# Down-projection of a convolutional FFN: where the residual sums, the bank reads and the operand sums are done

## The chip, the core and the metric

The kernel runs on one core of a Trainium2 chip. The metric is the device time of one execution in microseconds. Engines are called PE (TensorE), DVE (VectorE), ACT (ScalarE) and POOL (GpSimd); SP is the queue that issues the DMAs.

## What is computed

The program is one transformer layer on 1024 tokens of 1024 features. A Hyena mixer comes first, then the FFN of this case. Cut to what matters here:

```python
def conv_ffn(u, w_up, conv_w, conv_b, w_down, rows, cols):
    a, g = jnp.split(u @ w_up, 2, axis=-1)
    g = grid_dwconv(g, conv_w, conv_b, rows, cols)
    return (jax.nn.silu(g) * a) @ w_down
...
x = x + g2 * conv_ffn(modulate(rmsnorm(x, norm_g[i, 1]), sh2, sc2), *ffn_p, rows, GRID_W)
return rmsnorm(x, final_g)
```

The hidden width is 2816. All of it is float32: each float32 operand is split into a high and a low part, and a product is three matmuls.

## The kernel before, in words

The last stage, `ffn_down`, multiplies the hidden activations u (2816 x 1024 tokens, kept in DRAM as `du`) by w_down (2816 x 1024, `in_ffn_w_down_dram`). The product is made with seven block products instead of eight (the Strassen-Winograd scheme). Tokens, output features and the 2816 rows of the contraction are each cut in two halves. A product P1 to P7 runs over k = 0 to 10, blocks of 128 contraction rows, and for each k over four groups j of 128 tokens. So a step (p, k) is 4 x 3 = 12 matmuls of 128x128 by 128x512, and the stage has 77 steps. Four PSUM banks `bA` (named dA in the trace) take P1, P6, P7 and P4 one after the other; four banks `bB` (dB) take P2, P5 and P3. P6, P7 and P4 add onto what stands in bA: after P1 and P6 it is the sum called U2 here, after P7 it is U3, and P4 is added to that. So U2 and U3 have to be read out of bA before the next product changes it. The four quarters of the output are C11 (P1 + P2), C12 (U2 + P5 + P3; P3 is added onto P5 in bB), C22 (U3 + P5) and C21 (U3 + P4). In words of the code: C11 and C12 make tokens 0 to 511 (lo and hi features), C21 and C22 make tokens 512 to 1023.

The order of the steps is `dseq`, written out in `down_start`. P1 and P2 are mixed, then P6 and P5, then P7 k 0 and 1, P3 mixed with P7 k 2 to 4, P7 k 5 to 10, and P4. For every step, `down_load` issues DMAs from SP into a ring of raw tiles `dr` (13 tiles early, 11 from P5 k 7 on, 7 for P4), and `down_prep` makes the operands:

- for P5 it adds two tiles on POOL (line 1176), subtracts two on DVE (line 1177), and after the split writes two cached sums c for later products (lines 1203 and 1204);
- for P7 it makes one difference on POOL (line 1185) and one on DVE (line 1186); for P3 one on DVE (line 1189); for P4 one on POOL (line 1192);
- then `split` rounds each operand to its high part dh on ACT (line 62) and subtracts to get the low part dl on DVE (line 63).

A raw tile is free for the next DMA when its last reader is done. All the queues are in order: an instruction that waits holds those behind it on the same engine. The order on each engine is set by a scheduler when the program is built, not by the order of the lines alone.

The other work of the stage is the output. When a product is complete its banks are read: P1 to tiles p1 and P6 to tiles u2 by ACT (line 1300 for U2), P5 to tiles p5 by ACT (line 1304), P2, P3 and P7 by DVE, each adding the part stored before (lines 1307, 1315 and 1311). Then small jobs follow, popped one by one between the steps: `c11` multiplies by the gate g2 and adds the residual x1, both on POOL (line 1245, eight instructions); `c22` does the same for C22 on POOL (lines 1256 and 1251) with a square and its row sum on ACT; `c12` does it for C12 on DVE (lines 1265 and 1266) with squares on ACT (line 1268), then a mean, a reciprocal root (`rstd`, lines 354 to 362) and the final scaling (line 1276) with the output DMA. The tail is C21: for the last four k of P4 the loop runs j by j, and after each j DVE multiplies the bank by g2 (line 1332), adds the residual (line 1333), ACT squares, `rfin` makes the reciprocal root and DVE scales 1024 columns (line 1340) for a 512 KB output DMA; the last j is scaled in two halves, one on ACT (line 1343), one on DVE (line 1345).

Of the kernel before, what the change touches and what calls it, by code (L numbers as in the profile page):

```python
# [47 lines left out]
class Kern:  # L48
# [1167 lines left out]
    def ffn_down(self):  # L1216
# [30 lines left out]
        def c22(j, t):  # L1247
            y = lambda: self.x1[4 + j][:, hi]

            def last():  # L1250
                gt(out=y(), in0=y(), in1=t, op=ALU.add)
                self.sq(4 + j, 1, y(), t)
                if j == 3:
                    gt(out=y(), in0=y(), in1=fg[:, hi], op=ALU.mult)

            return [lambda: gt(out=t, in0=t, in1=g2[:, hi], op=ALU.mult), last]
# [24 lines left out]
        for n in range(N - LAST):  # L1281
# [37 lines left out]
            if vjobs and n % 3:  # L1319
                vjobs.pop(0)()  # L1320
        while vjobs or gjobs:
            for q in (gjobs, vjobs):
                if q:
                    q.pop(0)()
        for j in range(4):
            for n in range(N - LAST, N):
# [1 line left out]
            t = 4 + j
            y = self.x1[t]
            o = op.tile([128, 512], F32, tag="ot", name=f"dt{j}", bufs=2)  # L1330
            jk = op.tile([128, 512], F32, tag="nt", name=f"dj{j}", bufs=2)
            vt(out=o, in0=self.bA[j], in1=g2[:, lo], op=ALU.mult)  # L1332
            vt(out=y[:, lo], in0=y[:, lo], in1=o, op=ALU.add)  # L1333
            self.sq(t, 0, y[:, lo], jk)
# [2 lines left out]
            r = self.rfin(t)
            dst = a["out"][t * 128:t * 128 + 128]
            if j < 3:
                nc.vector.scalar_tensor_tensor(out=y, in0=y, scalar=r, in1=fg, op0=ALU.mult, op1=ALU.mult)  # L1340
                nc.sync.dma_start(out=dst, in_=y)
                continue
            nc.scalar.activation(out=y[:, hi], in_=y[:, hi], func=AF.Copy, scale=r)
            nc.sync.dma_start(out=dst[:, hi], in_=y[:, hi])
            nc.vector.tensor_scalar(out=y[:, lo], in0=y[:, lo], scalar1=r, scalar2=None, op0=ALU.mult)
            nc.sync.dma_start(out=dst[:, lo], in_=y[:, lo])

    def sq(self, t, h, y, junk):
        if t not in self.ssf:
            self.ssf[t] = self.op.tile([128, 2], F32, tag=f"ss2{t}", name=f"ssf{t}")  # L1350
        self.nc.scalar.activation(out=junk, in_=y, func=AF.Square, accum_out=self.ssf[t][:, h:h + 1])

    def rfin(self, t):
        ss = self.ssf[t]
        s1 = self.op.tile([128, 1], F32, tag="ss1", name=f"sst{t}", bufs=2)
        self.nc.vector.tensor_tensor(out=s1, in0=ss[:, 0:1], in1=ss[:, 1:2], op=ALU.add)
        return self.rstd(s1, 1, f"rf{t}")
# [158 lines left out]
```

## Time and profile before

| | us |
|---|---|
| median of 3 runs | 1305.76 (1305.61 to 1305.9) |
| the profiled execution's own time | 1301.95 |
| its span, first to last instruction | 1300.2 |
| busy: PE, DVE, ACT, POOL | 1232.0, 1063.9, 744.0, 353.2 |
| mean granted TensorE clock | 0.987 of 2.4 GHz |

Times in the rows are microseconds from the start of the span. A row of the timeline has the start, the time from the first start to the last end of the instructions that it merges, the engine, the line, the operation, the tiles written and read, and their count; in square brackets stands how long the engine was idle before, and what ended that. Instructions are pipelined: the next one starts some 0.08 us before the end of the one ahead on DVE, so the pace is a little shorter than the duration. A DMA row of SP shows the issue only. POOL spans are rough.

### The profile page before, as it was taken

What the parts mean: (1) busy time and instruction counts of PE and PEld (TensorE: products, weight loads), DVE (VectorE), ACT (ScalarE), POOL (GpSimd) and SP (SyncE); (2) the same over time, 40 slices, a digit from 0 to 9 for tenths busy, and PEclk for the clock granted to TensorE, in tenths of its full rate; (3) what the DMA queues carried; (4) which work ended last, traced back from release to release, by engine and by line L of the source; (5) the groups of instructions that cost most, each with busy time, mean ns of one, the idle gap of its engine ahead of it and who ended that gap; (6) DMA issues with size and microseconds to landing.
All of it is one profiled execution on the core that took longest, in us unless ns stands there. A gap on an engine that the chain in (4) does not pass through costs nothing. (4 is left out here: it accounts for less than half of the span.)

```text
span 1300.2 us, 16048 instructions
## 1 busy us (share of the span) xinstructions
PE 1232.0 (95%) x5368; PEld 971.7 (75%) x5368; DVE 1063.9 (82%) x1351; ACT 744.0 (57%) x1215; POOL 353.2 (27%) x292
## 2 busy tenths in 40 slices
PE   7999989999899999999989999999999999998976
PEld 2687767777677777878768878888888878886865
DVE  7899875578786998796989998788778798977996
ACT  4798866677676878553644444444544454425442
POOL 2000011012100210000086445455445301521461
PEclk9999999999999999999989999999999999999988
DMA  9555699989989997543124431222222388646542
GB/s 339 191 156 156 209 287 285 275 251 269 270 253 301 273 302 263 175 154 128 51 83 129 161 129 65 98 81 76 87 81 82 130 286 307 232 154 219 197 144 97
DMA packets 112400, 241.35 MB, mean 186 GB/s; under 512 B 12436, under 2 KB 25620, under 8 KB 112318
## 3 DMA queue, kind: packets, MB, share of 16 engines
q1 hardware_dynamic: 96790, 226.83, 53.4%
q0 software_dynamic: 14848, 13.39, 4.9%
q8 instruction: 42, 0.69, 0.2%
q14 instruction: 40, 0.33, 0.1%
q10 hardware_dynamic: 680, 0.12, 0.0%
HBM read 186.29 MB, written 54.00 MB: 185 GB/s over the span
## 5 line engine op out<-in xcount | busy, mean ns | idle before, releaser
L1010 DVE SCALAR_TENSOR_TENSOR facc<-fpad,v_ffn_conv_w,facc 128x1024 f32<-128x1024 f32 x176 | 225.2, 1285 | 22.8 <-ACT facc L1005 19.2
L62 ACT ACTIVATE dh<-dr 128x512 fp32r<-128x512 f32 x132 | 75.7, 623 | 64.0 <-PE dB L58 23.4
L63 DVE TENSOR_TENSOR dl<-dr,dh 128x512 fp32r<-128x512 f32 x132 | 102.8, 825 | 4.2 <-ACT dh L62 4.0
L507 POOL DMA_DIRECT2D k_b<-in_k_b_dram x64 | 34.0, 532 | 263.6 <-PE ks L59 177.3
L973 POOL TENSOR_TENSOR s<-wrua 128x512 f32<-128x512 f32 x21 | 29.3, 1396 | 188.2 <-DVE s12l L963 95.6
L57 PE MATMUL dA<-dh,dh 128*128 128x512 f32 x176 | 69.7, 396 | 8.7 <-DVE p5fpad L1311 7.7
L58 PE MATMUL dA<-dl,dh 128*128 128x512 f32 x176 | 69.2, 393 | 2.0 <-DVE dl L63 2.0
L963 POOL TENSOR_TENSOR s43l<-s,s43h 128x1024 fp32r<-128x1024 f32 x21 | 50.4, 2399 | 68.5 <-ACT s43h L962 68.5
L59 PE MATMUL dA<-dh,dl 128*128 128x512 f32 x176 | 68.9, 392 | 0.0
L58 PE MATMUL dB<-dl,dh 128*128 128x512 f32 x132 | 52.2, 395 | 5.1 <-DVE dl L63 5.1
L59 PE MATMUL dB<-dh,dl 128*128 128x512 f32 x132 | 51.9, 393 | 0.0
L57 PE MATMUL dB<-dh,dh 128*128 128x512 f32 x132 | 51.9, 393 | 0.0
L58 PE MATMUL op<-wlo,qh 128*128 128x512 f32 x128 | 50.3, 393 | 0.0
L57 PE MATMUL op<-who,qh 128*128 128x512 f32 x128 | 50.0, 393 | 0.0
L59 PE MATMUL op<-who,ql 128*128 128x512 f32 x128 | 49.9, 390 | 0.0
L1005 ACT ACTIVATE facc<-fpad,v_ffn_conv_b,v_ffn_conv_w 128x1024 f32<-128x1024 f32 x22 | 26.6, 1210 | 37.4 <-DVE fpad L1073 37.3
L57 PEld LDWEIGHTS dA<-dh,dh 128*128 128x128 f32 x176 | 33.5, 191 | 16.4 <-issue 8.1
L286 DVE SCALAR_TENSOR_TENSOR macc<-mw,scl,macc 128x1024 f32<-128x1024 f32 x28 | 38.1, 1361 | 9.4 <-DMA mw<-in_mod_w_dram 9.2
L507 POOL DMA_DIRECT2D k_bi<-in_k_bi_dram x32 | 17.1, 534 | 103.3 <-PE zd L59 47.6
L962 ACT ACTIVATE s12h<-s 128x1024 fp32r<-128x1024 f32 x21 | 22.3, 1061 | 39.6 <-PE s L58 35.3
L974 POOL TENSOR_TENSOR s<-s,wrug 128x512 f32<-128x512 f32 x21 | 42.8, 2039 | 1.5
L573 ACT ACTIVATE who<-wro,invn 128x512 fp32r<-128x512 f32 x32 | 21.8, 717 | 37.1 <-PE op L59 28.7
(585 smaller groups left out, 4050.4 us busy)
## 6 DMA issues: line engine op xcount, KB each, us to landing
dr<-du SPq DMA_DIRECT2D x66, 256.0 KB, 3.7
dr<-in_ffn_w_down_dram SPq DMA_DIRECT2D x66, 256.0 KB, 4.6
mw<-in_mod_w_dram SPq DMA_DIRECT2D x32, 512.0 KB, 4.6
wrin<-in_hy_w_in_dram SPq DMA_DIRECT2D x24, 512.0 KB, 6.4
wrug<-in_ffn_w_up_dram SPq DMA_DIRECT2D x22, 512.0 KB, 3.4
wrua<-in_ffn_w_up_dram SPq DMA_DIRECT2D x22, 512.0 KB, 4.7
du<-fs SPq DMA_DIRECT2D x22, 512.0 KB, 2.6
mw<-in_mod_w_dram SPq DMA_DIRECT2D x32, 256.0 KB, 6.5
```

The source lines that it names most:

```text
L57: mm(out=out, lhsT=lh, rhs=rh, start=start, stop=False, **kw)
L58: mm(out=out, lhsT=lh, rhs=rl, start=False, stop=False, **kw)
L59: mm(out=out, lhsT=ll, rhs=rh, start=False, stop=stop, **kw)
L62: self.nc.scalar.activation(out=hi, in_=src, func=AF.Copy)
L63: self.nc.vector.tensor_tensor(out=lo, in0=src, in1=hi.bitcast(F32), op=ALU.subtract)
L286: nc.vector.scalar_tensor_tensor(out=acc, in0=w, scalar=self.scl[:, kt:kt + 1], in1=acc, op0=ALU.mult, op1=ALU.add)
L507: self.nc.gpsimd.dma_start(out=b, in_=self.a[name][k2])
L963: eng.tensor_tensor(out=l, in0=src, in1=h.bitcast(F32), op=ALU.subtract)
L973: tt(out=s12[:, lo], in0=a[:, lo], in1=a[:, hi], op=ALU.add)
L974: tt(out=s12[:, hi], in0=s12[:, lo], in1=g[:, lo], op=ALU.subtract)
L1005: nc.scalar.activation(out=av, in_=pad[:, 1:17, 1:65], func=AF.Identity, scale=self.cw[:, b, 4:5], bias=self.cb[:, b:b + 1])
L1010: nc.vector.scalar_tensor_tensor(out=av, in0=pad[:, dy:dy + 16, dx:dx + 64], scalar=self.cw[:, b, i:i + 1], in1=av, op0=ALU.mult, op1=ALU.add)
```

## The change

- The differences of P7 (line 1185) and P4 (line 1192) move from POOL to DVE.
- C11: each group also gets its square (ACT) and its product with the final gain `fg` (POOL) at once: three POOL jobs each, where it was two.
- `pre`: after P6, U2 times g2 and the sum with the residual are done at once on POOL, two instructions for each of four groups; after P5 the same for P5 and a residual half `xh` that is loaded for it.
- P7's and P3's banks are read by the product with g2 (DVE, PSUM and SBUF operands) into a tile of its own, so that the stored first part is not needed at the read; one sum is left for each group, on POOL for C22 and on DVE for C12.
- C12's mean, root and scaling are popped in P4 only; the scaling is half on ACT, half on DVE.
- The tail's `rfin` takes the mean's factor into the square and has five DVE instructions instead of seven; hi halves are scaled by ACT and lo halves by DVE, each with a 256 KB DMA, and the fourth group's chain is put ahead of the third's.
- The residual loads of tokens 512 to 1023 become lo halves (256 KB) and, earlier, hi halves (256 KB).

```diff
         elif p == 7:
             a, b = r[0]
-            gt(out=a, in0=a, in1=self.cache[k][0], op=ALU.subtract)
+            vt(out=a, in0=a, in1=self.cache[k][0], op=ALU.subtract)
             vt(out=b, in0=self.cache[k][1], in1=b, op=ALU.subtract)
...
         else:
             a, b = r[0]
-            gt(out=b, in0=b, in1=self.cache[k][1], op=ALU.subtract)
+            vt(out=b, in0=b, in1=self.cache[k][1], op=ALU.subtract)
...
+        def square(j, h, t):
+            nc.scalar.activation(out=t, in_=self.x1[j][:, (lo, hi)[h]], func=AF.Square, accum_out=ss[:, h, j:j + 1])
+
         def c11(j, t):
             y = self.x1[j][:, lo]
-            return [lambda: gt(out=t, in0=t, in1=g2[:, lo], op=ALU.mult), lambda: gt(out=y, in0=y, in1=t, op=ALU.add)]
...
+            def add():
+                gt(out=y, in0=y, in1=t, op=ALU.add)
+                square(j, 0, t)
+
+            return [lambda: gt(out=t, in0=t, in1=g2[:, lo], op=ALU.mult), add, lambda: gt(out=y, in0=y, in1=fg[:, lo], op=ALU.mult)]
+
+        def pre(t, x, y):
+            return [lambda: gt(out=t, in0=t, in1=g2[:, hi], op=ALU.mult), lambda: gt(out=y, in0=x, in1=t, op=ALU.add)]
+
+        def c22(j, y, t):
+            def add():
+                gt(out=y, in0=y, in1=t, op=ALU.add)
+                self.sq(4 + j, y, t)
+
+            return add, lambda: gt(out=y, in0=y, in1=fg[:, hi], op=ALU.mult)
...
             def first(j):
-                t, y = u2[j], self.x1[j]
-                vt(out=t, in0=t, in1=g2[:, hi], op=ALU.mult)
-                vt(out=y[:, hi], in0=y[:, hi], in1=t, op=ALU.add)
...
+                y = self.x1[j][:, hi]
+                vt(out=y, in0=y, in1=u2[j], op=ALU.add)
+                square(j, 1, u2[j])
...
+            if (p, k) == (5, 7):
+                xh = [op.tile([128, 512], F32, tag=("ot", "nt")[j // 2], name=f"xh{j}", bufs=2) for j in range(4)]
+                for j in range(4):
+                    nc.sync.dma_start(out=xh[j], in_=self.dx[4 + j][:, hi])
...
                     for j in range(4):
                         nc.scalar.activation(out=u2[j], in_=self.bA[j], func=AF.Copy)
+                        y = self.x1[j][:, hi]
+                        gjobs += pre(u2[j], y, y)
                 elif p == 5:
                     p5 = four(("fpad0", "fpad1"), "p5")
                     for j in range(4):
                         nc.scalar.activation(out=p5[j], in_=self.bB[j], func=AF.Copy)
+                        gjobs += pre(p5[j], xh[j], p5[j])
...
                 elif p == 7:
                     for j in range(4):
-                        vt(out=p5[j], in0=self.bA[j], in1=p5[j], op=ALU.add)
-                    gjobs += [f for j in range(4) for f in c22(j, p5[j])]
+                        vt(out=xh[j], in0=self.bA[j], in1=g2[:, hi], op=ALU.mult)
+                    gjobs += [f for fs in zip(*[c22(j, p5[j], xh[j]) for j in range(4)]) for f in fs]
                 elif p == 3:
                     for j in range(4):
-                        vt(out=u2[j], in0=self.bB[j], in1=u2[j], op=ALU.add)
+                        vt(out=u2[j], in0=self.bB[j], in1=g2[:, hi], op=ALU.mult)
                     vjobs += c12(u2)
             if gjobs:
                 gjobs.pop(0)()
-            if vjobs and n % 3:
+            if vjobs and n % 3 and (p == 4 or len(vjobs) > 5):
                 vjobs.pop(0)()
...
+        qs = {}
         for j in range(4):
             for n in range(N - LAST, N):
                 self.down_mm(n, [j])
...
+            qs[j] = front(j)
             if j == 3:
...
+                back(3, qs[3])
+            if j:
+                back(j - 1, qs[j - 1])
...
+    def rfin(self, t, q):
+        nc, vv = self.nc, self.nc.vector
+        v, r, n = (self.cp.tile([128, 1], F32, tag=f"rs_{x}", name=f"rf{t}{x}", bufs=2) for x in "vrt")
+        vv.scalar_tensor_tensor(out=v, in0=q, scalar=EPS, in1=self.ssf[t], op0=ALU.add, op1=ALU.add)
+        nc.scalar.activation(out=r, in_=v, func=AF.Sqrt)
+        vv.reciprocal(out=r, in_=r)
+        vv.scalar_tensor_tensor(out=n, in0=r, scalar=v, in1=r, op0=ALU.mult, op1=ALU.mult)
+        vv.tensor_scalar(out=n, in0=n, scalar1=-0.5, scalar2=1.5, op0=ALU.mult, op1=ALU.add)
+        vv.tensor_tensor(out=r, in0=r, in1=n, op=ALU.mult)
+        return r
```

`front(j)` is the multiplication by g2, the residual sum and the square of tail group j; `back(j, q)` is its root, the two scalings and the two output DMAs.

How the built program orders this is shown at three places. In the rows, dr_7_0 is a raw tile of block k = 7, dh_4_0 and dl_4_0 are the split halves of an operand of k = 4, c_3 a cached sum of k = 3, x1r the residual tiles, p1fpad the stored P1 and macc the gate g2.

POOL after the reads of P2, from the third C11 job on, before:

```order
L1245 TENSOR_TENSOR p1fpad_9813<-p1fpad_9813,macc_7509 128x512
L1245 TENSOR_TENSOR p1fpad_9814<-p1fpad_9814,macc_7509 128x512
L1245 TENSOR_TENSOR x1r_9490<-x1r_9490,p1fpad_9813 128x512
L1245 TENSOR_TENSOR x1r_9492<-x1r_9492,p1fpad_9814 128x512
L1245 TENSOR_TENSOR p1fpad_9814<-p1fpad_9814,macc_7509 128x512
L1176 TENSOR_TENSOR dr_7_0_10067<-dr_7_0_10067,dr_7_2_10071 128x512
L1245 TENSOR_TENSOR x1r_9494<-x1r_9494,p1fpad_9814 128x512
L1176 TENSOR_TENSOR dr_8_0_10122<-dr_8_0_10122,dr_8_2_10126 128x512
```

and with the change, from the sixth C11 job on:

```order
L1255 TENSOR_TENSOR x1r_9489<-x1r_9489,fg 128x512
L1252 TENSOR_TENSOR x1r_9493<-x1r_9493,p1fpad_9815 128x512
L1255 TENSOR_TENSOR p1fpad_9815<-p1fpad_9815,macc_7509 128x512
L1255 TENSOR_TENSOR x1r_9491<-x1r_9491,fg 128x512
L1255 TENSOR_TENSOR x1r_9493<-x1r_9493,fg 128x512
L1252 TENSOR_TENSOR x1r_9495<-x1r_9495,p1fpad_9815 128x512
L1176 TENSOR_TENSOR dr_7_0_10070<-dr_7_0_10070,dr_7_2_10074 128x512
L1255 TENSOR_TENSOR x1r_9495<-x1r_9495,fg 128x512
L1176 TENSOR_TENSOR dr_8_0_10126<-dr_8_0_10126,dr_8_2_10130 128x512
L1176 TENSOR_TENSOR dr_9_0_10181<-dr_9_0_10181,dr_9_2_10185 128x512
L1176 TENSOR_TENSOR dr_10_0_10237<-dr_10_0_10237,dr_10_2_10241 128x512
L1258 TENSOR_TENSOR u2junk<-u2junk,macc_7509 128x512
```

P5's sum of k = 7 stood behind seven C11 instructions and stands behind eleven; the sixteen `pre` instructions (line 1258) follow the sum of k = 10 in one row, and lines 1185 and 1192, 22 instructions, are gone from POOL.

ACT in the same stretch, before:

```order
L62 ACTIVATE dh_3_0_10019<-c_3_9987 128x512
L62 ACTIVATE dh_3_1_10023<-c_3_9988 128x512
L62 ACTIVATE dh_4_0_10074<-c_4_10042 128x512
L62 ACTIVATE dh_4_1_10078<-c_4_10043 128x512
L62 ACTIVATE dh_5_0_10129<-c_5_10097 128x512
L62 ACTIVATE dh_5_1_10133<-c_5_10098 128x512
```

and with the change:

```order
L62 ACTIVATE dh_3_0_10021<-c_3_9989 128x512
L1246 ACTIVATE p1fpad_9814,ss_9385<-x1r_9489 128x512
L62 ACTIVATE dh_3_1_10025<-c_3_9990 128x512
L1246 ACTIVATE p1fpad_9814,ss_9385<-x1r_9491 128x512
L1246 ACTIVATE p1fpad_9815,ss_9385<-x1r_9493 128x512
L62 ACTIVATE dh_4_0_10077<-c_4_10045 128x512
L62 ACTIVATE dh_4_1_10081<-c_4_10046 128x512
L1246 ACTIVATE p1fpad_9815,ss_9385<-x1r_9495 128x512
L62 ACTIVATE dh_5_0_10133<-c_5_10100 128x512
```

Four squares of C11, each a reader of a POOL sum, now stand between the splits of P6's operands.

DVE ahead of the read of P7's banks (dA), before:

```order
L1271 TENSOR_TENSOR s_10911<-ss_10910 128x4
L354 TENSOR_SCALAR rf4v<-s_10911 128x4
L63 TENSOR_TENSOR dl_5_0_11130<-dr_5_0_10970,dh_5_0_11129 128x512
L63 TENSOR_TENSOR dl_5_1_11134<-dr_5_0_10970,dh_5_1_11133 128x512
L357 RECIPROCAL rf4r<-rf4r 128x4
L359 TENSOR_TENSOR rf4t<-rf4r 128x4
L360 TENSOR_TENSOR rf4t<-rf4t,rf4v 128x4
L361 TENSOR_SCALAR rf4t<-rf4t 128x4
L63 TENSOR_TENSOR dl_6_0_11154<-dr_6_0_10998,dh_6_0_11153 128x512
L1311 TENSOR_TENSOR p5fpad_10510<-dA_9375,p5fpad_10510 128x512
```

and with the change:

```order
L357 RECIPROCAL rf4r<-rf4r 128x4
L359 TENSOR_TENSOR rf4t<-rf4r 128x4
L360 TENSOR_TENSOR rf4t<-rf4t,rf4v 128x4
L1192 TENSOR_TENSOR dr_10_0_11132<-dr_10_0_11132,c_10_10368 128x512
L63 TENSOR_TENSOR dl_5_0_11137<-dr_5_0_10998,dh_5_0_11136 128x512
L63 TENSOR_TENSOR dl_5_1_11141<-dr_5_0_10998,dh_5_1_11140 128x512
L361 TENSOR_SCALAR rf4t<-rf4t 128x4
L362 TENSOR_TENSOR rf4r<-rf4r,rf4t 128x4
L1283 SCALAR_TENSOR_TENSOR x1r_9489<-x1r_9489,rf4r,fg 128x512
L1283 SCALAR_TENSOR_TENSOR x1r_9491<-x1r_9491,rf4r,fg 128x512
L1326 TENSOR_TENSOR xh_10379<-dA_9375,macc_7509 128x512
```

C12's root stands ahead of the bank read in both; with the change two of its four scalings do too, and so do all eleven differences of P4. Between the first read of P3's banks and the first of P7's, DVE has 30 instructions before and 32 with the change.

## Rows read from the trace of the kernel before

**Rows 1.** Windows: us, busy time of each engine (instructions), clock, DMA share, GB/s.
```profile
1150.00:1200.00 50.00, 43.04 (x180) 33.97 (x178) 35.55 (x49) 22.69 (x42) 11.25 (x9) 0.97 0.59 190
...
1250.00:1300.00 50.00, 31.73 (x132) 25.86 (x132) 40.02 (x68) 14.05 (x34) 20.92 (x13) 0.84 0.23 92
```

**Rows 2.** Timeline of PE in the stage, the matmuls with idle time before them.
```profile
1169.53 0.50 PE L58 MATMUL dB<-dl,dh 128*128 128x512 f32 x1 [0.61 <-DVE dl L63]
...
1180.42 0.50 PE L58 MATMUL dB<-dl,dh 128*128 128x512 f32 x1 [2.44 <-DVE dl L63]
...
1186.88 0.50 PE L58 MATMUL dA<-dl,dh 128*128 128x512 f32 x1 [1.98 <-DVE dl L63]
...
1200.16 0.50 PE L58 MATMUL dB<-dl,dh 128*128 128x512 f32 x1 [2.08 <-DVE dl L63]
...
1256.85 0.76 PE L57 MATMUL dA<-dh,dh 128*128 128x512 f32 x1 [7.66 <-DVE p5fpad L1311]
1257.41 0.63 PE L58 MATMUL dA<-dl,dh 128*128 128x512 f32 x1
```

**Rows 3.** Timeline of DVE while POOL works on C11.
```profile
1119.22 2.47 DVE L1307 TENSOR_TENSOR p1fpad<-dB,p1fpad 128x512 f32<-128x512 f32 x4
...
1122.98 3.48 DVE L63 TENSOR_TENSOR dl<-c,dh 128x512 fp32r<-128x512 f32 x2
...
1138.39 0.68 DVE L1204 TENSOR_TENSOR c<-dr,dr 128x512 f32<-128x512 f32 x1
```

**Rows 4.** Timeline of POOL in the same stretch.
```profile
1121.21 1.29 POOL L1245 TENSOR_TENSOR p1fpad<-p1fpad,macc 128x512 f32<-128x512 f32 x1
...
1124.16 3.44 POOL L1245 TENSOR_TENSOR p1fpad<-p1fpad,macc 128x512 f32<-128x512 f32 x2
...
1132.67 1.74 POOL L1176 TENSOR_TENSOR dr<-dr,dr 128x512 f32<-128x512 f32 x1
```

**Rows 5.** Timeline of ACT, the split of P6's k = 4.
```profile
1122.30 1.16 ACT L62 ACTIVATE dh<-c 128x512 fp32r<-128x512 f32 x2 [1.56 <-issue]
```

**Rows 6.** Timeline of SP: two issues for P5's k = 8 and 9.
```profile
1139.15 0.33 SPq L1142 DMA_DIRECT2D dr<-du  x1
...
1151.43 0.93 SPq L1142 DMA_DIRECT2D dr<-du  x2
```

**Rows 7.** Timeline of DVE, P5's k = 9 and 10.
```profile
1158.40 0.69 DVE L1203 TENSOR_TENSOR c<-dr 128x512 f32<-128x512 f32 x1 [3.17 <-POOL dr L1176]
...
1166.48 1.78 DVE L1204 TENSOR_TENSOR c<-dr,dr 128x512 f32<-128x512 f32 x1
```

**Rows 8.** Timeline of DVE from the end of P5 to the first steps of P3.
```profile
1181.12 1.27 DVE L1186 TENSOR_TENSOR dr<-c,dr 128x512 f32<-128x512 f32 x1 [0.76 <-DMA dr<-in_ffn_w_down_dram]
...
1196.60 1.22 DVE L1186 TENSOR_TENSOR dr<-c,dr 128x512 f32<-128x512 f32 x1 [2.46 <-DMA dr<-in_ffn_w_down_dram]
1197.74 2.36 DVE L63 TENSOR_TENSOR dl<-dr,dh 128x512 fp32r<-128x512 f32 x2
```

**Rows 9.** Timeline of ACT, the reads of P6's and P5's banks.
```profile
1180.19 1.06 ACT L1300 ACTIVATE u2junk<-dA 128x512 f32<-128x512 f32 x2
...
1184.18 1.58 ACT L1304 ACTIVATE p5fpad<-dB 128x512 f32<-128x512 f32 x3
```

**Rows 10.** Timeline of DVE from P7's last difference to the read of P7's banks.
```profile
1216.23 20.43 DVE L63 TENSOR_TENSOR dl<-dr,dh 128x512 fp32r<-128x512 f32 x21
1236.58 1.27 DVE L1315 TENSOR_TENSOR u2junk<-dB,u2junk 128x512 f32<-128x512 f32 x2
...
1256.02 2.48 DVE L1311 TENSOR_TENSOR p5fpad<-dA,p5fpad 128x512 f32<-128x512 f32 x4
```

**Rows 11.** Timeline: a load for P4 on SP, and the POOL difference that waits for it.
```profile
1228.00 0.33 SPq L1142 DMA_DIRECT2D dr<-du  x1
...
1231.65 1.45 POOL L1192 TENSOR_TENSOR dr<-dr,c 128x512 f32<-128x512 f32 x1 [0.85 <-DMA dr<-in_ffn_w_down_dram]
```

**Rows 12.** Timeline of the tail: last matmul, last bank read, last output DMA.
```profile
1288.19 0.39 PE L59 MATMUL dA<-dh,dl 128*128 128x512 f32 x1
...
1290.22 0.68 DVE L1332 TENSOR_TENSOR dt<-dA,macc 128x512 f32<-128x512 f32 x1
...
1296.89 0.38 SPq L1344 DMA_DIRECT2D out_dram<-x1r  x1
```

More of the change, by code (lines that the diff above doesn't have):

```diff
@@ L1241, in ffn_down @@
         gjobs, vjobs = [], []
+        ss = op.tile([128, 2, 4], F32, tag="ss4", name="ss4")
+        def square(j, h, t):
+            nc.scalar.activation(out=t, in_=self.x1[j][:, (lo, hi)[h]], func=AF.Square, accum_out=ss[:, h, j:j + 1])
         def c11(j, t):
             y = self.x1[j][:, lo]
-            return [lambda: gt(out=t, in0=t, in1=g2[:, lo], op=ALU.mult), lambda: gt(out=y, in0=y, in1=t, op=ALU.add)]
[L1247 to L1256, printed above, removed]
+            def add():
[9 more added lines that the diff above has]
+            return add, lambda: gt(out=y, in0=y, in1=fg[:, hi], op=ALU.mult)
         def c12(u2):
-            ss = op.tile([128, 2, 4], F32, tag="ss4", name="ss4")
             s1 = op.tile([128, 4], F32, tag="s14", name="s14")
@@ L1274, in last @@
             def last(j):
-                y = self.x1[j]
-                nc.vector.scalar_tensor_tensor(out=y, in0=y, scalar=r[0][:, j:j + 1], in1=fg, op0=ALU.mult, op1=ALU.mult)
+                y, rj = self.x1[j], r[0][:, j:j + 1]
+                nc.scalar.activation(out=y[:, lo], in_=y[:, lo], func=AF.Copy, scale=rj)
+                nc.vector.scalar_tensor_tensor(out=y[:, hi], in0=y[:, hi], scalar=rj, in1=fg[:, hi], op0=ALU.mult, op1=ALU.mult)
                 nc.sync.dma_start(out=a["out"][j * 128:j * 128 + 128], in_=y)
@@ L1287, in ffn_down @@
                     resid(t)
-            if (p, k) == (7, NK - 2):
+            if (p, k) == (4, 2):
                 for t in range(4, 8):
-                    resid(t)
+                    self.x1[t] = self.xtile(t, [128, 512], f"x1r_{t}")
+                    nc.sync.dma_start(out=self.x1[t], in_=self.dx[t][:, lo])
+            if (p, k) == (5, 7):
+                xh = [op.tile([128, 512], F32, tag=("ot", "nt")[j // 2], name=f"xh{j}", bufs=2) for j in range(4)]
+                for j in range(4):
+                    nc.sync.dma_start(out=xh[j], in_=self.dx[4 + j][:, hi])
             self.down_mm(n)
@@ L1324, in ffn_down, with front, back @@
                     q.pop(0)()
+        def front(j):
+            y = self.x1[4 + j]
+            o = op.tile([128, 512], F32, tag="ot", name=f"dt{j}", bufs=2)
+            jk = op.tile([128, 512], F32, tag="nt", name=f"dj{j}", bufs=2)
+            vt(out=o, in0=self.bA[j], in1=g2[:, lo], op=ALU.mult)
+            vt(out=y, in0=y, in1=o, op=ALU.add)
+            q = op.tile([128, 1], F32, tag=f"sl{j}", name=f"sl{j}")
+            nc.scalar.activation(out=jk, in_=y, func=AF.Square, scale=1.0 / 32, accum_out=q)
+            return q
+        def back(j, q):
+            t, y, z = 4 + j, self.x1[4 + j], p5[j]
+            if j == 3:
+                vt(out=y, in0=y, in1=fg[:, lo], op=ALU.mult)
+            r = self.rfin(t, q)
+            dst = a["out"][t * 128:t * 128 + 128]
+            nc.scalar.activation(out=z, in_=z, func=AF.Copy, scale=r)
+            nc.sync.dma_start(out=dst[:, hi], in_=z)
+            if j == 3:
+                nc.vector.tensor_scalar(out=y, in0=y, scalar1=r, scalar2=None, op0=ALU.mult)
+            else:
+                nc.vector.scalar_tensor_tensor(out=y, in0=y, scalar=r, in1=fg[:, lo], op0=ALU.mult, op1=ALU.mult)
+            nc.sync.dma_start(out=dst[:, lo], in_=y)
+        qs = {}
         for j in range(4):
@@ L1327, in ffn_down @@
                 self.down_mm(n, [j])
[L1328 to L1334, printed above, removed]
-            if j == 3:
-                vt(out=y[:, lo], in0=y[:, lo], in1=fg[:, lo], op=ALU.mult)
@@ L1337, in ffn_down @@
[L1337 to L1357, printed above, removed]
+            qs[j] = front(j)
@@ new lines, in ffn_down, with sq @@
+            if j == 3:
+                back(3, qs[3])
+            if j:
+                back(j - 1, qs[j - 1])
+    def sq(self, t, y, junk):
+        nc = self.nc
+        v = self.ssf[t] = self.op.tile([128, 1], F32, tag=f"ss2{t}", name=f"ssf{t}")
+        nc.scalar.activation(out=junk, in_=y, func=AF.Square, scale=1.0 / 32, accum_out=v)
+    def rfin(self, t, q):
[8 more added lines that the diff above has]
+        return r
```

2 lines of the change are left out of this document (removed).

## The prediction

> **What bounds the kernel now.** I read the windows first, for who is busy where; then the timeline of PE, for the places where it stands still; then those of the engines that release it. Over most of the down-projection PE has work (43.0 of the 50 us from 1150 on, and of the rest some is the places below [rows 1]). What can move the end are therefore the few places where a matmul waits [rows 2]: 0.61 and 2.44 us in P5's last steps, 1.98 and 2.08 us around the start of P7 and P3, 7.66 us ahead of P4; and the tail, from the last matmul to the end of the span. Every one of these waits ends with a DVE instruction. So the question is what the change does to DVE's row in front of these places. What DVE adds to them reaches the end one for one, unless a later gap shrinks.
>
> Two prices are needed throughout. A DVE instruction of 128x512 with both operands in SBUF takes 0.68 us alone [rows 3, 12], and in a row one follows another every 0.60, as the four bank reads show (2.48 for four, the last of them 0.68, so three steps of 0.60) [rows 10]. While POOL works back to back, two of them take 3.48 [rows 3], one of them 1.78 [rows 7], that is a pace of 1.70. POOL's instruction takes 1.29 alone and about 1.74 in that company [rows 4]. So each POOL instruction that meets DVE's SBUF work costs DVE 1.70 - 0.60 = **1.10 us**. The Trainium skill states a stricter rule (SBUF — State Buffer, "SBUF: two separate sides"): VectorE and GpSimd share a port pair behind an exclusive lock that is held for a whole instruction. By that a POOL instruction would cost DVE its full 1.29; the trace gives 1.10, and I take the trace.
>
> **The sum, part by part.**
>
> *A. C11.* POOL gets twelve instructions where it had eight, and P5's sum of k = 7 (line 1176) now stands behind eleven of them, not seven. While they run DVE goes at the slow pace: four more cost 4 x 1.10 = 4.4 us. The four squares stand between P6's splits on ACT; two splits take 1.16 [rows 5], so a square that waits for its POOL sum holds the next split for about 0.5. Together 4.9: the cached sum (line 1204) at 1138.39 [rows 3] comes at about 1143.3. It frees a raw tile, and SP issues the next load 0.08 after its end, at 1139.15 [rows 6]. From there to P5's k = 9 I find no slack: SP's next pair leaves at 1151.43 [rows 6], DVE waits 3.17 for POOL's sum at 1158.40 [rows 7], and PE for DVE at 1169.53 and 1180.42 [rows 2]. One collision goes: the cached sum at 1166.48 took 1.78 [rows 7] next to P7's difference on POOL, which is now on DVE: -1.1. **+3.8**. Bounds: 2, if half of the four meet DVE where it would wait anyway; 5, without the last gain.
>
> *B. `pre`.* U2 is read by ACT from 1180.19 and P5 from 1184.18 [rows 9], and behind P5's sum of k = 10 POOL has nothing but the sixteen `pre` instructions. 16 x 1.74 is 27.8 us in one run, from about 1184.5 (with A) to 1212. Just there DVE has the chain that PE waits for: from the end of P5's last split, 1181.12 - 0.76 = 1180.36, to the second split of P3's k = 1, 1197.74 + 2.36 = 1200.10 [rows 8], it is 19.7 us for 19 instructions, 11.4 of it work and 8.3 waits and collisions (0.76 and 2.46 of wait stand in the rows). With the change it has 21, since two differences of P7 come from POOL: 21 x 0.60 + 16 x 1.10 = 30.2 us, in which the waits are absorbed. **+10.4**, paid by PE ahead of P7's k = 0 and P3's k = 0 and 1. From below, if half of the sixteen fall into the waits and the rest behind the stretch: 21 x 0.60 + 8 x 1.10 = 21.4, +1.7; from above with 1.29 each: 33.2, +13.5. I take the middle price since the two pairs in rows 3 and 4 are just this case, DVE dense beside POOL dense. By the skill's rule (same section) it would be the upper end.
>
> *C. Read of P7's banks.* Before, from 1216.23 on DVE has 21 splits in 20.43 us [rows 10] (21 x 0.60 and seven collisions with line 1192 at 1.10 make 20.3), then P3's reads and 19.4 us to the read at 1256.02 [rows 10], after which PE can start P4: the 7.66 [rows 2]. Together 39.8 us. With the change the seven collisions go, but the differences stand in DVE's own row. A raw tile of P4's k is given back by a pair of splits, and between that pair and the difference only one difference and one pair stand (1.8 us), while the load takes 1231.65 - 1228.00 = 3.65 us [rows 11]. So two steps take 3.65 + 0.1 + 3 x 0.60 = 5.55, one 2.75, and the stretch 8.5 such steps, 23.4. From P3's reads to P7's the order has 25 full and some 7 small instructions, 25 x 0.60 + 7 x 0.2 = 16.4. Sum 39.8, as before: **0**. The mean of C12 is ahead of the read in both, as the order shows, so it gives nothing. Bounds: without the load's wait, 28 x 0.60 + 16.4 = 33.2, -6.6, with which the gap closes to about 1.0, and with it goes most of the clock's fall that follows it: the first P4 matmuls stand 0.56 apart [rows 2], half the pace (the 1.2 level); six of them cost 6 x 0.28, about 1.6 more: -8.2. Upwards +3, the four other differences and two scalings each meeting a wait of about half a microsecond.
>
> *D. Tail.* Before: last matmul 1288.19, last bank read 1290.22, last DMA issued 1296.89 [rows 12], end of the span 1300.2. Two small DVE instructions go from the root, the multiplication with both halves becomes one half on ACT and one on DVE, the fourth group is ahead of the third's. By the instructions I place the last issue at 6.6 after the end of the last matmul, where it was 1296.89 - 1288.58 = 8.3; with the same 3.3 from there to the end of the span the tail is 9.9 where it was 11.6. **-1.7**; bounds -1.0 (the third group's DMA, now last, ends later) and -2.6.
>
> *E. Rest.* The halves of the residual loads have the same bytes; what POOL gets rid of (22 differences) counts in A to C. The clock falls in long PE idle time, as it does ahead of P4: hidden where PE waits for DVE anyway, 0, at most +2.
>
> Sum: 3.8 + 10.4 + 0 - 1.7 = **+12.5 us**. The profiled execution takes 1301.95 and would take 1314.4; the median is 1305.76, 3.8 above it, and I add the +12.5 there: **1318.3**. Of this kernel about 0.2% (2.6 us) can be told from no change.
>
> **Rivals.**
>
> 1. *The gap ahead of P4 closes*, A and B true: 12.5 - 8.2 = +4.3, 1310.1. For it: seven collisions and a PSUM-with-SBUF product that needs no stored part. Against: the loads' loop of 5.55 for two steps. Chance 0.2.
>
> 2. *The other side, faster.* DVE has slack ahead of P7: POOL's `pre` work falls into its waits (8.3 us of 19.7) and behind the stretch. Place: DVE between 1180 and 1200. B then is 1.7, and since DVE comes early to P7's end the gap closes too: 3.8 + 1.7 - 8.2 - 1.7 = -4.4, 1301.4. It decides from the point where at most eight of the sixteen meet DVE; with A hidden as well 1297.6. Against: rows 3, where DVE never got a free turn while POOL was dense. Chance 0.17.
>
> 3. *The gap ahead of P4 closes halfway and half of B is hidden*, or the change does not do what it says beyond the tail: within 2.6 us of 1305.8. The order shows the mean where it was, so that part does nothing. Chance 0.08.
>
> 4. *The whole instruction locks*: 1.29 in A and B makes +3.1 + 0.8, and the differences of P4 wait: up to 1325. The Trainium skill's section above says it so; the 1.70 pace of rows 3 and 7 speaks against the full price. Chance 0.1.
>
> Forecast: 0.45. Together faster 0.17, same 0.08, slower 0.75. The range leaves out the far end of rival 2 and above rival 4: 1302 to 1324; the forecast's own, with A from 2 to 5, B from about 7 to 13.5, D, is 1313 to 1323.
>
> **What would show it.** POOL line 1258 sixteen times without a gap at about 1.7 each, and DVE at 1.7 beside it; PE idle some 11 us ahead of P7's k = 0 and 5 ahead of P3's k = 0; SP's issue for P5's k = 8 about 5 later; ahead of P4 again 7 to 8 us, released by line 1326; from the last matmul to the end of the span 9.6 to 10.2 where it was 11.6. The forecast is wrong if DVE instructions beside `pre` take 0.68, if PE starts P7 less than 6 us late, or if P4 starts within 3 us of P7's end.

## The result and the profile after

The changed kernel took 1322.2 us in the median of four runs (1313.72 to 1324.62), the kernel before 1305.83; the ratio is **1.0112** (95% interval 1.0080 to 1.0143), slower by 1.1%; 1318.3 was forecast, 1302 to 1324. In a second measurement the ratio was 1.0115 (1.0083 to 1.0147).

The profiled execution has a span of 1322.8 us, 22.6 more than before, and not all of that is the change's. The point from which times are counted here is the start of the 924th matmul from the end (77 steps of twelve): it stands at 1064.53 us; before it stood at 1058.36. The first matmul of the down-projection itself starts 2.7 us ahead of that point in every profile (1061.81, before 1055.64), because twelve matmuls that write another tile (s) are mixed in behind it; no difference changes by this. The code ahead of it is the same, and in fourteen profiles of this case the point lay anywhere from 1055.2 to 1065.9, without regard to the kernel. So 6.2 us are of the execution, and what is called the stage from here on goes from that point to the end of the span: **258.3 us, before 241.8**. The pieces:

| us from that point | before | changed | changed, again | forecast of the difference |
|---|---|---|---|---|
| P7's k = 0 starts (A) | 125.91 | 129.27 | 128.79 | +3.8 |
| from there to P3's k = 2 (B) | 18.51 | 30.40 | 30.61 | +10.4 |
| from there to P4's k = 2 (C) | 61.15 | 64.09 | 61.63 | 0 |
| from there to the last matmul's end | 24.64 | 24.64 | 24.64 | 0 |
| tail (D) | 11.60 | 9.91 | 9.93 | -1.7 |
| stage | 241.81 | 258.32 | 255.60 | +12.5 |

The timeline of PE, the matmuls with idle time before them, answers to [rows 2]:

```profile
1171.39 0.50 PE L58 MATMUL dB<-dl,dh 128*128 128x512 f32 x1 [1.63 <-DVE dl L63]
1179.79 0.58 PE L58 MATMUL dB<-dl,dh 128*128 128x512 f32 x1 [2.42 <-DVE dl L63]
1191.15 0.50 PE L58 MATMUL dB<-dl,dh 128*128 128x512 f32 x1 [1.30 <-DVE dl L63]
1204.57 0.79 PE L58 MATMUL dA<-dl,dh 128*128 128x512 f32 x1 [10.38 <-DVE dl L63]
1214.70 0.49 PE L58 MATMUL dB<-dl,dh 128*128 128x512 f32 x1 [1.47 <-DVE dl L63]
1221.55 0.50 PE L58 MATMUL dB<-dl,dh 128*128 128x512 f32 x1 [1.10 <-DVE dl L63]
...
1279.99 0.77 PE L57 MATMUL dA<-dh,dh 128*128 128x512 f32 x1 [9.40 <-DVE xh L1326]
```

The releasers are the same, and there is one new large wait, 10.38 us in P7's k = 0. Beside it POOL runs `pre` (its timeline; [rows 4] has the prices before):

```profile
1190.57 1.68 POOL L1258 TENSOR_TENSOR u2junk<-u2junk,macc 128x512 f32<-128x512 f32 x1 [13.36 <-ACT u2junk L1312]
...
1207.30 3.42 POOL L1258 TENSOR_TENSOR p5fpad<-p5fpad,macc 128x512 f32<-128x512 f32 x2
...
1215.87 1.62 POOL L1258 TENSOR_TENSOR p5fpad<-xh,p5fpad 128x512 f32<-128x512 f32 x1
```

and DVE, from the cached sum of k = 7 (line 1204) to the second split of P3's k = 1 (its timeline, as [rows 3, 8]):

```profile
1149.77 0.68 DVE L1204 TENSOR_TENSOR c<-dr,dr 128x512 f32<-128x512 f32 x1
...
1189.81 1.29 DVE L63 TENSOR_TENSOR dl<-dr,dh 128x512 fp32r<-128x512 f32 x2
...
1192.72 1.78 DVE L1186 TENSOR_TENSOR dr<-c,dr 128x512 f32<-128x512 f32 x1
1194.43 3.42 DVE L63 TENSOR_TENSOR dl<-dr,dh 128x512 fp32r<-128x512 f32 x2
1197.77 3.41 DVE L1189 TENSOR_TENSOR dr<-dr,c 128x512 f32<-128x512 f32 x2
...
1220.21 1.29 DVE L63 TENSOR_TENSOR dl<-dr,dh 128x512 fp32r<-128x512 f32 x2
```

For sixteen POOL instructions in one row, 1190.57 to 1217.49, DVE goes at 1.70 an instruction, and goes back to 0.60 behind them.

### The profile page after: what moved, and what is told of

It reads as the page before. It is cut to its first block, busy times and chain, and to the rows that moved or that the text cites. A ratio compares the mean times of both kernels' runs of the same rounds, so it can differ in the third digit from the quotient of the medians.

```text
span 1322.8 us, 16066 instructions
## 1 busy us (share of the span) xinstructions
PE 1239.9 (94%) x5368; PEld 976.5 (74%) x5368; DVE 1067.2 (81%) x1361; ACT 748.2 (57%) x1222; POOL 346.6 (26%) x289
## 4 chain that ended last, share of the span: by engine, by line
PE 68%; DVE 10%; DMA 10%; issue 6%; ACT 3%; POOL 1%; SPq 0%; ACTq 0%; DVEq 0%; POOLq 0%
PE s L57 5%; PE s L58 5%; PE s L59 5%; PE uz L57 3%; PE uz L58 3%; PE uz L59 3%; DVE dl L63 3%; DMA k_b<-in_k_b_dram 2%; PE op L57 2%; PE op L58 2%; PE op L59 2%; PE dA L57 2%; PE dA L59 2%; PE dA L58 2%; DMA dr<-du 2%
## 5 line engine op out<-in xcount | busy, mean ns | idle before, releaser
L57 PE MATMUL dA<-dh,dh 128*128 128x512 f32 x176 | 71.0, 403 | 10.6 <-DVE xh L1326 9.4
L58 PE MATMUL dA<-dl,dh 128*128 128x512 f32 x176 | 71.0, 404 | 10.4 <-DVE dl L63 10.4
L58 PEld LDWEIGHTS dA<-dl,dh 128*128 128x128 f32 x176 | 34.5, 196 | 18.4 <-DVE dl L63 11.1
L507 POOL DMA_DIRECT2D k_bi<-in_k_bi_dram x32 | 17.1, 536 | 103.4 <-PE zd L59 47.6
```

The costliest lines, as they stand in the source:

```text
L57: mm(out=out, lhsT=lh, rhs=rh, start=start, stop=False, **kw)
L58: mm(out=out, lhsT=lh, rhs=rl, start=False, stop=False, **kw)
L507: self.nc.gpsimd.dma_start(out=b, in_=self.a[name][k2])
```

## The experiments

Read from each kernel's profile: starts of P5's k = 10, P7's k = 0 and P3's k = 2 (us from the point named above), idle time ahead of P4, tail, whole stage; beside it the measured ratio to the kernel before. There is one profile for each row, and the order on the engines is made anew at each build, so small differences of a piece mean little: the two profiles of the changed kernel differ by 2.3 us ahead of P4, and tail_only and act_read_late, whose edits lie behind P3's k = 2, have 16.7 and 17.4 us from P7's k = 0 to there, where the kernel before has 18.5.

| kernel | P5 k 10 | P7 k 0 | P3 k 2 | idle P4 | tail | stage | ratio (95% interval) |
|---|---|---|---|---|---|---|---|
| before | 119.2 | 125.9 | 144.4 | 7.66 | 11.60 | 241.8 | 1 |
| changed | 124.9 | 129.3 | 159.7 | 9.40 | 9.91 | 258.3 | 1.0112 (1.0080, 1.0143) |
| again | 124.5 | 128.8 | 159.4 | 7.10 | 9.93 | 255.6 | 1.0115 (1.0083, 1.0147) |
| pre_left_out | 125.4 | 133.2 | 149.1 | 7.53 | 9.91 | 245.6 | 0.9995 (0.9965, 1.0025) |
| pre_dve | 124.8 | 130.3 | 150.3 | 4.07 | 9.80 | 242.4 | 1.0007 (0.9988, 1.0026) |
| c11_undone | 118.0 | 122.8 | 153.4 | 4.93 | 10.14 | 247.0 | 1.0053 (1.0019, 1.0087) |
| c11_late_squares | 122.8 | 129.9 | 159.5 | 6.40 | 9.81 | 254.1 | 1.0083 (1.0057, 1.0109) |
| mean_late | 124.0 | 128.5 | 158.7 | 6.50 | 9.80 | 254.3 | 1.0083 (1.0054, 1.0112) |
| tail_only | 119.7 | 126.4 | 143.1 | 7.48 | 10.00 | 239.8 | 0.9984 (0.9959, 1.0010) |
| diffs_only | 117.6 | 121.8 | 140.8 | 4.57 | 11.60 | 236.3 | 0.9955 (0.9935, 0.9975) |
| tail_diffs | 118.8 | 123.4 | 141.3 | 7.23 | 10.00 | 239.0 | 0.9962 (0.9940, 0.9983) |
| act_read_late | 119.8 | 126.8 | 144.2 | 2.32 | 10.00 | 245.1 | 1.0030 (1.0010, 1.0050) |
| act_read_diffs_late | 117.8 | 124.2 | 141.0 | 6.50 | 10.01 | 243.8 | 0.9984 (0.9962, 1.0007) |
| repaired | 118.4 | 125.5 | 140.7 | 5.46 | 9.81 | 234.6 | 0.9934 (0.9905, 0.9963) |

**again**: no edit.

> The changed kernel once more. In its first profile the stage began 6.2 us later than before (first matmul at 1064.53, was 1058.36), in a part of the program whose code is the same, and the stage itself took 258.3 us to the end of the span (was 241.8). Theory: the 16.5 in the stage belongs to the change and comes again within 1 us, the 6.2 ahead of it varies from execution to execution, so the first matmul lies anywhere from 1058 to 1065. Rival: the 6.2 come with the changed program (its buffers lie elsewhere), then the first matmul stands at 1064 to 1065 again.

The first matmul stood at 1059.83, the stage took 255.6. The 6.2 us are not the change's. Of the 16.5 in the stage 13.8 came again, where at least 15.5 were expected; what moved is above all P4's idle time, from 9.40 to 7.10. (The expectation calls the point of counting the first matmul; that one stood at 1057.11.)

**pre_left_out** and **pre_dve**: what the sixteen instructions cost, and what they cost on the other engine.

```diff
-            return [lambda: gt(out=t, in0=t, in1=g2[:, hi], op=ALU.mult), lambda: gt(out=y, in0=x, in1=t, op=ALU.add)]
+            return []
```

> The changed kernel without the sixteen POOL instructions of pre (so U2 and P5 lack the gate and the residual). Collision theory: the stretch from P7's k = 0 to P3's k = 1, where the lateness grew from 3.2 to 15.1 us, loses 10 to 12 of it; the stage takes 246 to 248 and the kernel is 10 to 12 us faster than the changed one. Rival, that the two differences of P7 that DVE took over and their loads set the stretch: at most 2 x 0.6 plus a wait of 1 to 2, so the stage stays at 255 or more, 0 to 3 faster.

```diff
-            return [lambda: gt(out=t, in0=t, in1=g2[:, hi], op=ALU.mult), lambda: gt(out=y, in0=x, in1=t, op=ALU.add)]
+            return [lambda: vt(out=t, in0=t, in1=g2[:, hi], op=ALU.mult), lambda: vt(out=y, in0=x, in1=t, op=ALU.add)]
```

> The changed kernel with the sixteen instructions of pre on DVE instead of POOL; the stage of the changed kernel took 258.3 and 255.6 us in two profiles. Collision theory: beside DVE's dense chain a POOL instruction costs DVE 1.10 us, more than the 0.60 that the same work costs on DVE itself; so doing all of it on DVE is faster, by 16 x 0.5 = 8 us and up to 12 where the work falls into DVE's waits: stage 244 to 249. Rival, that DVE is simply short of time there: sixteen more instructions of 0.6 on it make the stage 10 longer, 265 or more, or leave it at 255 to 258.

Left out, the way from P7's k = 0 to P3's k = 2 falls from 30.5 to 15.9 us, and the stage to 245.6: the rival of the moved differences is out. P7's k = 0 itself comes about 4 us later there, so P3's k = 2 gains 10.4 to 10.6. On DVE the same work is nearly free: 20.0 us for that way, P3's k = 2 only 1.2 later than without the work, and the whole loss of the kernel gone (ratio 1.0007), more than the 8 to 12 expected. Of the 13.2 to 15.9 that the stage gains, 9.1 to 9.4 stand at P3's k = 2; the rest lies behind it, mostly ahead of P4 (4.07), and no run shows its cause. PE's timeline, of pre_left_out and of pre_dve:

```profile
1198.77 0.50 PE L58 MATMUL dA<-dl,dh 128*128 128x512 f32 x1 [1.22 <-DVE dl L63]
```

```profile
1190.92 0.80 PE L58 MATMUL dA<-dl,dh 128*128 128x512 f32 x1 [3.37 <-DVE dl L63]
```

The timeline of DVE of pre_dve shows why:

```profile
1194.60 1.29 DVE L63 TENSOR_TENSOR dl<-dr,dh 128x512 fp32r<-128x512 f32 x2
1195.81 1.29 DVE L1258 TENSOR_TENSOR u2junk<-u2junk,macc 128x512 f32<-128x512 f32 x2
1197.01 1.29 DVE L1258 TENSOR_TENSOR x1r<-x1r,u2junk 128x512 f32<-128x512 f32 x2
```

Two take 1.29, one follows another every 0.60, and the splits beside them keep their pace (1.29 for two); and the order puts them behind the splits that PE waited for (P7's k = 0 went on at 1190.92), while POOL, with nothing else in its queue, begins the moment U2 is read. `pre` on POOL at a later place was not run, so how much of the gain is price and how much is place stays open.

**c11_undone** and **c11_late_squares**: the third C11 job, and its parts.

```diff
-            return [lambda: gt(out=t, in0=t, in1=g2[:, lo], op=ALU.mult), add, lambda: gt(out=y, in0=y, in1=fg[:, lo], op=ALU.mult)]
+            return [lambda: gt(out=t, in0=t, in1=g2[:, lo], op=ALU.mult), lambda: gt(out=y, in0=y, in1=t, op=ALU.add)]
...
+                square(j, 0, u2[j])
                 square(j, 1, u2[j])
```

> The changed kernel with C11's third job and early square undone (eight POOL instructions, squares and full scaling in C12). Theory: PE's lateness at the end of P5 (3.2 us) goes, and since pre starts by that much earlier the rest moves with it: 2.5 to 3.5 us faster than the changed kernel in the stage (255 to 256). Rival: PE waits for DVE beside pre anyway, so what comes earlier at P5 is waited for at P7: 0 to 1 faster.

c11_late_squares has only the squares moved so (its row sums are then of values already multiplied by `fg`).

> The changed kernel with C11's squares back in C12, its twelve POOL instructions kept. With them undone altogether, P5's k = 10 started at 118.0 us of the stage; in the changed kernel at 124.9 and 124.5. Theory: four more POOL instructions ahead of P5's sum of k = 7 make up most of it, 4 x 1.1 to 4 x 1.7 = 4.4 to 6.8: k = 10 at 122.4 or later. Rival: the squares that hold ACT's splits of P6 are the cause, then 118 to 120.

Undone, P7's k = 0 comes 6.0 us earlier than in the repeated run and P3's k = 2 as much (PE's timeline):

```profile
1182.69 0.50 PE L58 MATMUL dB<-dl,dh 128*128 128x512 f32 x1 [1.75 <-DVE dl L63]
...
1196.11 0.80 PE L58 MATMUL dA<-dl,dh 128*128 128x512 f32 x1 [10.37 <-DVE dl L63]
```

The 10.37 us beside `pre` stay, so the two costs add; the rival that one covers the other is out. The size was expected at 2.5 to 3.5 and is 6, in the stage with P4's shorter idle time 8.7 to 11.4. With only the squares moved, P5's k = 10 gains 1.7 to 2.1 of 6.4 to 6.9 and P3's k = 2 nothing (159.5): the larger part is the four POOL instructions, as expected.

**mean_late**: C12's mean is made to depend on the bank read.

```diff
+                vt(out=z, in0=xh[3][:, 0:4], in1=xh[3][:, 0:4], op=ALU.subtract)
                 vt(out=s1, in0=ss[:, 0], in1=ss[:, 1], op=ALU.add)
+                vt(out=s1, in0=s1, in1=z, op=ALU.add)
```

> The changed kernel with C12's mean made to depend on the read of P7's banks, so that it, the root and two scalings really stand behind the read on DVE (they took about 3 us ahead of it). Theory: the idle time ahead of P4 (9.4 and 7.1 in two profiles) falls by 2 to 3 us and the stage with it, to 253 to 255. Rival: DVE waits there for loads of P4, and what goes from its row turns into waiting: no change, 255.5 to 258.5.

The idle time ahead of P4 was 6.50, against 9.40 and 7.10 with a spread of its own of 2.3: 0.6 to 2.9 less, not clear of that spread. The stretch of DVE's row on which the edit acts, from the first read of P3's banks to the first of P7's, says more (DVE's timeline of mean_late):

```profile
1255.73 1.28 DVE L1333 TENSOR_TENSOR u2junk<-dB,macc 128x512 f32<-128x512 f32 x2
...
1271.65 2.48 DVE L1329 TENSOR_TENSOR xh<-dA,macc 128x512 f32<-128x512 f32 x4
```

It took 15.9 us, where the changed kernel has 17.1 and 16.9: the mean's place is worth 1.0 to 1.2 there, not 2 to 3.

**tail_only, diffs_only, tail_diffs**: single parts on the kernel before.

> The kernel before with the change's tail alone (shorter root, lo halves on DVE, hi halves on ACT, fourth group ahead of the third). Theory: 1.7 us faster than before, 1304.1, and 9.9 us from the last matmul to the end of the span (was 11.6). Rival: the last output DMA sets the end whatever the chain does, then within 0.5 of before, 1305.5.

> The kernel before with the differences of P7 and P4 on DVE and nothing else (stage before: 241.8; P7's k = 0 at 125.9 us from the stage's start, idle time ahead of P4 7.7). Theory: the move saves 1.10 - 0.60 at each collision and takes DVE's wait for POOL away, P7's k = 0 comes 2 to 3 us earlier as it did without the third C11 job (122.8); ahead of P4 the load's wait takes the collisions' place, the idle time there stays at 6 to 9: stage 238 to 240. Rival: 22 more instructions on DVE make both gaps longer: stage 243 or more.

> The kernel before with the change's tail and its differences on DVE, nothing else. Theory: the two parts lie in different stretches and add: 236.3 with the differences alone, less 1.6 of the tail: stage 234 to 235.5, the time 6 to 8 us under the kernel before. Rival: the tail's three added products of C22 on POOL meet DVE's sums ahead of the last group, and the gain of 1.6 is lost: stage 236 or more.

The tail is 1.6 us shorter (1.7 expected), but 0.7 us of it come back as a wait in P4's k = 7 (tail_diffs: 1.35), so the stage gains 2.0 together with what varies, and the runs' interval takes in 1. The differences on DVE are the one part that pays by itself: 5.5 us in the stage (1.8 to 3.8 expected), and ratio 0.9955. P3's k = 0 and 1 no longer wait; PE's timeline has in this stretch only

```profile
1181.92 0.50 PE L58 MATMUL dB<-dl,dh 128*128 128x512 f32 x1 [1.05 <-DVE dl L63]
1188.47 0.57 PE L58 MATMUL dA<-dl,dh 128*128 128x512 f32 x1 [3.50 <-DVE dl L63]
...
1254.57 0.76 PE L57 MATMUL dA<-dh,dh 128*128 128x512 f32 x1 [4.57 <-ACT dh L62]
```

With the tail added the time is the same within the intervals (0.9962). The stage, 239.0, misses the 234 to 235.5 expected: P7's k = 0 comes 1.6 later than with the differences alone, and P4's idle time is 7.23, where it was 4.57. That gap is the least steady piece: in the changed kernel's two profiles it differs by 2.3 us, 1.5 of it in DVE's waits for loads of P4 (8.4 and 6.9 us in all).

**act_read_late** and **act_read_diffs_late**: P7's banks copied out by ACT, on tail_only, with the mean behind; the second also with the differences on DVE.

```diff
-                        vt(out=p5[j], in0=self.bA[j], in1=p5[j], op=ALU.add)
+                        nc.scalar.activation(out=u3[j], in_=self.bA[j], func=AF.Copy)
```

> The kernel before with the change's tail, C12's mean behind the read, and P7's banks copied out by ACT (as P6's and P5's are), with one more sum of 128x512 on DVE per group behind it. Theory: PE waits ahead of P4 because DVE's row reaches the read late; ACT is not late there, so the idle time of 7.7 falls to 1 to 2.5, the clock stays up, and the stage takes 232 to 235 (before 241.8, with the tail alone 239.8). Rival: ACT's squares of C12 wait for DVE's sums and hold ACT's read as long: idle 5 or more, stage 237 to 240.

> As the kernel with ACT's read (tail, mean behind the read), and the differences of P7 and P4 on DVE. There POOL's four last differences of P4 took 14 us beside DVE's dense row and P4's k = 7 waited 6.8 us for them. Theory: on DVE they can't be held up that way; P7's k = 0 comes at about 122 us of the stage, the idle time ahead of P4 is 1 to 2.5 and none over 1 follows in P4: stage 229 to 232, about 10 us less than before. Rival: the late differences wait for their loads, which SP issues behind the residual's, and P4's k = 7 waits as it did: stage 235 or more, no better than the differences alone (236.3).

The first closed the gap as expected, 2.32 us, and lost it again: P4's k = 7 waited 6.8 us (and the time from P4's k = 2 to the last matmul's end went from 24.6 to 35.0). POOL's timeline there, ACT's, and the rows of DVE and PE at that wait:

```profile
1249.93 13.99 POOL L1192 TENSOR_TENSOR dr<-dr,c 128x512 f32<-128x512 f32 x4 [12.36 <-DMA dr<-in_ffn_w_down_dram]
1263.88 1.29 POOL L1257 TENSOR_TENSOR p5fpad<-p5fpad,macc 128x512 f32<-128x512 f32 x1
```

```profile
1257.41 0.60 ACT L1318 ACTIVATE u<-dA 128x512 f32<-128x512 f32 x1
1266.56 0.63 ACT L1369 ACTIVATE p5fpad<-x1r 128x512 f32<-128x512 f32 x1 [8.55 <-POOL x1r L1251]
```

```profile
1279.31 4.64 DVE L1282 SCALAR_TENSOR_TENSOR x1r<-x1r,rf4r,fg 128x1024 f32<-128x1024 f32 x3
...
1285.21 0.80 PE L58 MATMUL dA<-dl,dh 128*128 128x512 f32 x1 [6.07 <-DVE dl L63]
```

POOL's four differences took 14 us, then C22's sums came late, and ACT, in order, held P4's next splits behind C22's square for 8.55 us. On DVE three scalings of C12 (4.64) then stood ahead of the split that PE waited for. With the differences on DVE the second kernel has the same square in ACT's way, and ahead of the read ACT waits for C12's sums, which was the rival of the first:

```profile
1249.11 0.63 ACT L1271 ACTIVATE u2junk<-x1r 128x512 f32<-128x512 f32 x1 [8.94 <-DVE x1r L1269]
...
1259.19 1.55 ACT L1318 ACTIVATE u<-dA 128x512 f32<-128x512 f32 x3
...
1267.17 0.63 ACT L1369 ACTIVATE p5fpad<-x1r 128x512 f32<-128x512 f32 x1 [5.43 <-POOL x1r L1251]
```

Both miss; squares and scalings that could wait stand ahead of splits that could not.

**repaired**: the change with `pre` on DVE, C11 undone and the mean late, by the three edits above.

> The changed kernel with three parts put right: pre on DVE, C11 with its eight POOL instructions and no early square, C12's mean behind the bank read. Theory, by the parts measured apart: with pre on DVE the stage took 242.4; C11 undone took 6 us off it up to P5's k = 10 (118 instead of 124.8), the mean's place 0.5 to 3: stage 233.5 to 236, the time 5 to 8 us under the kernel before. Rival: the parts cover each other (what comes earlier at P5 is waited for at P7 or ahead of P4): stage 238 to 242, 0 to 4 under the kernel before.

234.6 us and a ratio of **0.9934** (0.9905 to 0.9963): 0.7% under the kernel before, within the expected bounds. The sum of the parts came out, though not piece by piece: against pre_dve P3's k = 2 comes 9.6 earlier, where C11 was to give 6, and the idle time ahead of P4 is 1.4 longer. It beats both kernels. The differences alone (0.9955) can't be told from it.

## Why the prediction held

The path was the one forecast: DVE held beside POOL, ahead of P7. The sum, 12.5, was too small: the stage grew by 16.5 and 13.8 us, the medians by 16.4 and 13.9. B gave 1.5 and 1.7 more than forecast, C 2.9 and 0.5, and A 0.4 and 0.9 less.

**B, the largest term, step by step.** The forecast gave DVE's chain from P5's last split to the second split of P3's k = 1 a time of 21 x 0.60 + 16 x 1.10 = 30.2 us. It ran from 1189.81 + 1.29 = 1191.10 to 1220.21 + 1.29 = 1221.50, 30.4 us; POOL took 26.9 where 27.8 stood. PE lost 11.9 and 12.1 there, forecast 10.4; most of the rest is that PE reached P7's k = 0 2.7 us behind P5's last split, where it had been 3.9 (see A). Leaving the work out gave back 10.4 to 10.6 at P3's k = 2. On price by the whole instruction (rival 4), DVE's pace of 1.70 beside `pre` is the row of before again, 1.10 a piece. The Trainium skill (SBUF — State Buffer, "SBUF: two separate sides") has the pair locked for the whole instruction; by that, as an estimate, this chain would take 16 x 1.29 + 12.6 = 33.2. The trace, 30.4, decides.

One of the signs missed: PE waited 1.47 us ahead of P3's k = 0, not about 5. Behind the 10.38 its matmuls stood 0.43 apart where 0.23 is usual, at a granted clock of 0.50 (the 1.2 GHz level) from 1204.60 to 1208.00, and so reached P3 later. As E had it, this cost nothing: PE still waited for DVE, 1.47 and 1.10, behind it.

**A** came out at +3.4 and +2.9 for 3.8, by two wrong sizes that cancel, which is luck. C11's addition is 6.0 to 6.4 us at P7's k = 0 (c11_undone), not 4.9, and the differences taken from POOL give back 4.2 there in diffs_only and 3.1 in c11_undone (0.5 in repaired, so the point varies), not 1.1. The forecast counted one collision. What else the differences cost there no run takes apart: in the kernel before ACT waited for them three times, 6.7 us in all. And 1.2 us is PE's clock, which E put at 0. The windows show the clock, the first of the kernel before, the others of the changed one:

```profile
1180.40:1184.30 3.90, 3.88 (x12) 3.02 (x12) 3.07 (x4) 3.90 (x9) 1.29 (x1) 0.67 0.79 251
...
1191.10:1193.80 2.70, 2.65 (x11) 2.17 (x12) 2.45 (x2) 2.70 (x6) 2.62 (x2) 1.00 0.75 234
...
1204.60:1208.00 3.40, 3.40 (x8) 2.72 (x9) 3.40 (x3) 0.00 (x0) 3.32 (x3) 0.50 0.50 154
```

In P5's k = 10 PE had waited 2.44 us before; the granted clock behind it had a mean of 0.67 (part of it at the 1.2 GHz level), and the eleven matmuls from there to P7's k = 0 took 3.85. With the change it had waited 1.30, the clock stayed at 1.00 (2.4 GHz), and they took 2.65. So P5's k = 10 came 5.7 late, and 1.1 less of wait and 1.2 less at the low clock left 3.4 at P7's k = 0. The mark named for A was right: the cached sum of k = 7 ended 5.2 later in the stage (1149.77 + 0.68 - 1064.53 = 85.92, before 80.71; forecast 4.9).

**C** was put at 0 and is +2.9 and +0.5. The working held within a microsecond or two: to P3's reads 25.1 us for 23.4 and from there to P7's 17.1 for 16.4, in the repeated run 23.6 and 16.9 (DVE's timeline of the changed kernel):

```profile
1237.02 1.28 DVE L63 TENSOR_TENSOR dl<-dr,dh 128x512 fp32r<-128x512 f32 x2
...
1249.40 0.69 DVE L1192 TENSOR_TENSOR dr<-dr,c 128x512 f32<-128x512 f32 x1 [3.09 <-DMA dr<-in_ffn_w_down_dram]
...
1255.23 0.69 DVE L1192 TENSOR_TENSOR dr<-dr,c 128x512 f32<-128x512 f32 x1 [2.13 <-DMA dr<-in_ffn_w_down_dram]
...
1262.07 1.28 DVE L1330 TENSOR_TENSOR u2junk<-dB,macc 128x512 f32<-128x512 f32 x2
...
1271.08 0.15 DVE L1277 TENSOR_TENSOR s<-ss 128x4 f32<-128x4 f32 x1
...
1279.16 2.48 DVE L1326 TENSOR_TENSOR xh<-dA,macc 128x512 f32<-128x512 f32 x4
```

The waits for loads stand in DVE's own row, 5.83 us from one to the second next (forecast 5.55): rival 1, the gap closing, fell to that. So what the seven collisions cost is gone and given back in those waits.

**D** was -1.7 and is -1.7. Last issue 1319.19 (SP's timeline), 6.3 after the last matmul's end of 1312.93; forecast 6.6.

```profile
1319.19 0.41 SPq L1362 DMA_DIRECT2D out_dram<-x1r  x1
```

Rival 2, slack in DVE ahead of P7, is contradicted by the 10.38 us; that work in DVE's own row, placed later, finds room there (pre_dve) was not seen. Rival 3 fell with the ratio.

## What to carry to other kernels

Work "moved off" a busy engine is only off it if the two don't slow each other: look up in the trace what the bound engine's instructions take while the other runs, and compare that surcharge (here 1.10 us) with doing the work there (0.60). An engine with an empty queue starts such work at once, even where a later place would do, so try it in the bound engine's own row behind what is waited for (price and place were not told apart here). When a bundle loses, its parts alone can still win: the differences did.
